# Causal mask on the tensor engine, q scaled before it is turned, and half of an output projection between heads

## The chip, the cores and the metric

The kernel runs on one core of a Trainium2 chip. The metric is the device time of one execution in microseconds (us). Five engines work side by side, each in its own fixed order of instructions: PE (matrix products and transposes), DVE (elementwise operations and reductions), ACT (activations and copies), POOL (elementwise operations) and SP (here it only issues DMAs). They wait for each other by semaphores. SBUF is the on-chip memory, PSUM the accumulator memory in banks of 2 KB a partition, into which PE writes. A change is timed by the median of several executions.

## The reference

The program is a trunk of two layers over x [512 tokens, 1024]. Each layer is a gated feed-forward block, a mixer, a cross attention to 256 memory tokens and another feed-forward block. The change touches layer 1's mixer alone:

```python
def _mla_mixer(h, positions, w_in, q_lora_g, kv_lora_g, w_uq, w_ukv, q_g, k_g, w_out):
    c_q, c_kv, k_r = jnp.split(h @ w_in, [512, 768], axis=-1)
    q = (_rmsnorm(c_q, q_lora_g) @ w_uq).reshape(b, s, 16, 96)
    kv = (_rmsnorm(c_kv, kv_lora_g) @ w_ukv).reshape(b, s, 16, 64 + 64)
    k_nope, v = kv[..., :64], kv[..., 64:]
    k = jnp.concatenate([k_nope, broadcast(k_r)], axis=-1)   # 64 + 32
    q = _rmsnorm(q, q_g); k = _rmsnorm(k, k_g)               # per head, over 96
    ... # rope on the last 32 of q and k
    sc = q @ k.T * 96 ** -0.5
    p = softmax(where(k_pos <= q_pos, sc, -inf))
    return (p @ v).reshape(b, s, 1024) @ w_out
```

There are 16 heads of 96 (q, k) and 64 (v) columns. The result is added to x, and the cross attention follows.

## The kernel before, in words

x lives feature-major on the chip, as eight tiles [128, 512]. Every large product runs as three passes of PE (lines 97 to 100, `mm3`): each operand is split into a high part, rounded to the multiplier's width (type fp32r), and a low part; the passes are high by high, low by high and high by low. Weights come in granules by DMA from SP's queue (L89); ACT makes their high part (L79), POOL or DVE the low part (L83).

**Layer 1's attention** is `mla_attn`. The 16 heads are in four groups of four. A group's projections are eight steps: four of q, one for each tile of 128 tokens (`proj_q`: a product of 384 columns into one of two banks "A", a copy, the squares on ACT at L681, their sums on DVE at L682), then four of k and v (`proj_kv`, 512 columns). After the last step come the sums' inverse roots (`rsqrt`), the scale of q by token and head (`sqr`, L663), and the normalized k (`ks`, L638 and L639; on DVE for group 0, on POOL for the others). 14 of the 32 steps run before the first head, the rest as filler between the parts of the heads, where the table FILL says how many steps stand at each of three places of a head.

**The loop over n = 0..16** does, in this order on PE: the scores of head n in three units of query blocks (512, then 384 + 128, then 256 columns; three PSUM banks "lg"); the transposes of head n-1's weights, units 0 and 1; filler; the transposes of unit 2; the turn of q and k for head n+2 (`turn`: four transposes each, L703); filler; the product with v (`values`, L808); filler. All transposes write one of two PSUM banks "pt". A bank is free again when it has been copied out: the weights' units 0 and 1 (wT0, wT1) by ACT at L795, unit 2 (wT2) by DVE at L797, q and k by both engines.

**A head's softmax**: DVE adds the mask to the diagonal blocks in PSUM (L760), reduces each row to its negative maximum (L765), multiplies that by the token's scale of q (L767); ACT takes the exponential with that scale and bias and sums the rows (L771); DVE inverts the sums (L773) and scales the rows (L777).

A scheduler sets the order of the instructions on each engine when the program is built, by its own costs. On PE the code fixes the order in addition (`queued`): what a part issues comes behind what was issued before it.

**The output projection** (`out_proj`) follows the loop: four pairs of output tiles, each pair in two halves of the contraction (o's tiles 0 to 3, then 4 to 7; one such tile holds two heads), 24 PE passes a half; then x += the result (L194), and the next norm's split and squares. The squares of the memory's tokens and its split (the next stage's preparation) are spread into the same time.

Of the kernel before, what the change touches and what calls it, by code (L numbers as in the profile page):

```python
# [8 lines left out]
F32R = mybir.dt.float32r  # L9
I32 = mybir.dt.int32  # L10
AF = mybir.ActivationFunctionType
ALU = mybir.AluOpType
# [14 lines left out]
class Trunk:  # L27
    """The residual stream xT lives feature-major on chip; every product runs as
    three fp32r passes over operands split exactly into a high and a low part."""

    def __init__(self, ctx, tc, a, stop=None):
# [10 lines left out]
        # PSUM: two banks stay through all phases, which start in their own banks and end in these two,  # L42
        # so that no phase's first product waits for the last one's evacuation
# [3 lines left out]
    def queued(self):  # L47
        """What the block issues on the tensor engine comes behind what it had before."""
        return self.tc.issue_after(self.pe.ins)
# [9 lines left out]
    # ---------------------------------------------------------------- pieces  # L59
    def constants(self):  # L60
# [3 lines left out]
        # the first weights ahead of x: their split takes longer  # L64
# [10 lines left out]
    def split(self, hi, lo, src, eng_hi="act", eng_lo="dve"):  # L75
        """hi = src rounded to the multiplier's width, lo = src - hi (exact)."""
# [8 lines left out]
    def gran(self, src, kt, cols, lo="pool"):  # L85
        """A weight granule [128, kt*cols] loaded and split."""
# [15 lines left out]
    def rsqrt(self, ssq, n, scale, eps, shape=None):  # L102
        """1/sqrt(ssq*scale + eps) on [128, n] by bit estimate and three Newton steps."""
# [13 lines left out]
    def prep(self, g, f):  # L117
        """Split gain*x_f for the next norm's consumers."""
# [12 lines left out]
    def squares(self, f):  # L131
        """Add the squares of x_f to the sums of the next norm."""
# [9 lines left out]
    def stats(self, pp, tag, bufs=None, bc=False):  # L142
        """rstd of every token: rc [128, NT] by token tile, and, if bc, rbc broadcast over partitions."""
# [28 lines left out]
    def out_half(self, ps, w, src, kh, first):  # L172
        """One half of the contraction of a pair of out_proj's output tiles, in steps."""
        wh, wl = self.gran(w, 4, 256)
        for m in range(2):
            for k in range(4):
                c = slice(m * P, (m + 1) * P)
                self.mm3(ps[m], (wh[:, k, c], wl[:, k, c]), src[4 * kh + k], first and k == 0, not first and k == 3)
                yield

    def out_proj(self, pp, tag, w, src, order, g, begun=None):
        """x += src @ w by pairs of output tiles; w in granules [pair*2 + khalf] of [128, 4, 256].
        begun: accumulators that hold the first half already."""
        nc = self.nc
        for mp in range(4):
            if begun and mp in begun:
                ps = begun[mp]
            else:
                ps = [self.psA() if mp in (0, 3) else self.t(pp, [P, S], tag) for _ in range(2)]
                self.run_all(self.out_half(ps, w[mp * 2 + order[0]], src, order[0], True))  # L190
            self.run_all(self.out_half(ps, w[mp * 2 + order[1]], src, order[1], False))
# [7 lines left out]
    # ---------------------------------------------------------------- FFN  # L199
# [43 lines left out]
    # ---------------------------------------------------------------- token-major products  # L243
    def tok_chunk(self, pp, tag, grans):
        """h @ w for 256 columns, token-major: two banks of [128, 2, 256]."""
# [11 lines left out]
    # ---------------------------------------------------------------- layer 0's mixer  # L257
# [15 lines left out]
    def sgu(self, p, pp, v, og):  # L273
# [8 lines left out]
        # only s <= t mixes: partition s, free t  # L282
# [50 lines left out]
    def stick(self, p, pp, v, ob, src):  # L333
        """Stick-breaking attention, scores as [key, query]: causal blocks only."""
        nc, a = self.nc, self.a
        # key block -> (unit, column of its queries j*128.. in the unit); units are one bank each
# [9 lines left out]
        # -1 where row key >= column key  # L346
# [3 lines left out]
        # far below every score where key >= query: no softplus there, and no weight  # L350
# [762 lines left out]
```

## Time and profile before

| | |
|---|---|
| median of 3 runs | 2326.71 us (2326.22 to 2329.08) |
| the profiled execution's span | 2328.0 us |
| PE / DVE / ACT / POOL busy | 98% / 44% / 38% / 39% of the span |
| granted TensorE clock in the stretches of layer 1's attention | 1.00 |
| layer 1's attention and its projections | about 1580 to 1750 us |
| output projection behind it, to its last pass | 1750 to 1783.6 us |

Times in rows are us from the start of the span, unless marked ns. A row of an instruction gives start, duration, engine, line, operation, output <- inputs, partitions and elements; in brackets the idle time of its engine before it and what ended it. A row of a group gives the count, the busy time in us with the mean of one in ns, and the idle time before the group's instructions. The windows give, for each stretch, its length, each engine's busy time with the count of its instructions, the granted clock, the DMA share and GB/s. A matmul's duration runs to its modelled end, so consecutive ones overlap in the rows: what one costs PE is the distance from its start to the next start.

### The profile page before, as it was taken

Reading aid. Unit: us, or ns where it says so; the run is one execution under the profiler, and the core shown is the slowest. Engines: PE = TensorE matmul, PEld = TensorE weight load, DVE = VectorE, ACT = ScalarE, POOL = GpSimd, SP = SyncE. Lnnn points to the kernel's source line nnn. Section 1 sums busy time; section 2 is a strip of 40 time slices with the busy share of each in tenths; the row PEclk is TensorE's granted clock in tenths of the full one; section 3 lists DMA queues with packets and bytes.
Section 4 is the critical chain, followed back from the end, with each engine's and each line's share of the span. In section 5 each row is a group of like instructions: output and inputs, shape, how many; then the busy total and the mean of one; then the engine's idle time right before and its main releaser. Section 6 shows DMA issues by size and latency. Waiting matters only on the chain. (4 is left out here: it accounts for less than half of the span.)

```text
span 2328.0 us, 28369 instructions
## 1 busy us (share of the span) xinstructions
PE 2274.4 (98%) x11152; PEld 1891.5 (81%) x11152; DVE 1018.2 (44%) x1830; ACT 875.1 (38%) x1448; POOL 903.4 (39%) x441
## 2 busy tenths in 40 slices
PE   7999999999999999999999999998999999999999
PEld 6888888977988788888878888897768887888887
DVE  5322433465745533133343133368886545430330
ACT  4222233355644332232332223346655443322321
POOL 4444444201242444444544444434212323445443
PEclk9999999999999999999999999999999999999999
DMA  4223323311431232332322332321103313323322
GB/s 152 92 87 113 92 82 118 92 46 47 134 110 55 83 99 81 110 100 83 108 90 83 108 100 86 99 80 57 37 19 119 127 55 91 91 79 111 100 81 92
DMA packets 67350, 208.65 MB, mean 90 GB/s; under 512 B 8592, under 2 KB 10640, under 8 KB 67216
## 3 DMA queue, kind: packets, MB, share of 16 engines
q1 hardware_dynamic: 67216, 206.83, 29.1%
q8 instruction: 88, 1.44, 0.3%
q14 instruction: 46, 0.38, 0.1%
HBM read 204.70 MB, written 2.10 MB: 89 GB/s over the span
## 5 line engine op out<-in xcount | busy, mean ns | idle before, releaser
L83 POOL TENSOR_TENSOR wl<-wr,wh 128x1024 fp32r<-128x1024 f32 (+2 forms) x382 | 850.6, 2227 | 1253.0 <-ACT wh L79 1188.8
L79 ACT CAST wh<-wr 128x1024 fp32r<-128x1024 f32 (+3 forms) x423 | 408.7, 966 | 1029.8 <-PE mm L99 540.7
L98 PE MATMUL mm<-hh,wh 128*128 128x512 f32 x1440 | 562.8, 391 | 6.6 <-ACT hh L125 6.6
L100 PE MATMUL mm<-hh,wl 128*128 128x512 f32 x1440 | 562.5, 391 | 0.9 <-POOL wl L83 0.9
L99 PE MATMUL mm<-hl,wh 128*128 128x512 f32 x1440 | 562.2, 390 | 0.5 <-DVE hl L126 0.5
L98 PEld LDWEIGHTS mm<-hh,wh 128*128 128x128 f32 x1440 | 271.5, 189 | 62.9 <-ACT hh L125 6.6
L100 PEld LDWEIGHTS mm<-hh,wl 128*128 128x128 f32 x1440 | 271.6, 189 | 57.6 <-POOL wl L83 1.3
L99 PEld LDWEIGHTS mm<-hl,wh 128*128 128x128 f32 x1440 | 271.3, 188 | 57.6 <-DVE hl L126 1.0
L98 PE MATMUL A<-ah,wh 128*128 128x512 f32 x704 | 277.4, 394 | 0.0
L100 PE MATMUL A<-ah,wl 128*128 128x512 f32 x704 | 276.0, 392 | 0.0
L99 PE MATMUL A<-al,wh 128*128 128x512 f32 x704 | 273.2, 388 | 0.0
L222 DVE TENSOR_TENSOR t<-mm,rbc 128x512 f32<-128x512 f32 x88 | 60.8, 691 | 390.5 <-PE mm L100 390.5
L234 DVE SCALAR_TENSOR_TENSOR x<-A,x 128x512 f32<-128x512 f32 x64 | 44.3, 691 | 354.3 <-PE A L100 354.3
L83 DVE TENSOR_TENSOR al<-t,ah 128x512 fp32r<-128x512 f32 x88 | 160.8, 1828 | 59.1 <-ACT ah L79 59.1
L100 PEld LDWEIGHTS A<-ah,wl 128*128 128x128 f32 x704 | 132.1, 188 | 31.0
L99 PEld LDWEIGHTS A<-al,wh 128*128 128x128 f32 x704 | 132.2, 188 | 29.6
L98 PEld LDWEIGHTS A<-ah,wh 128*128 128x128 f32 x704 | 132.3, 188 | 26.4
L220 DVE TENSOR_TENSOR t<-mm,rbc 128x512 f32<-128x512 f32 x88 | 60.9, 692 | 117.1 <-PE mm L100 110.8
L126 DVE SCALAR_TENSOR_TENSOR hl<-x,gc,hh 128x512 fp32r<-128x512 f32 x64 | 82.8, 1307 | 36.7 <-ACT hh L125 36.6
L98 PE MATMUL A<-hh,wh 128*128 128x512 f32 x224 | 91.6, 410 | 0.7 <-ACT hh L79 0.7
L99 PE MATMUL A<-hl,wh 128*128 128x512 f32 x224 | 90.0, 402 | 0.0
L100 PE MATMUL A<-hh,wl 128*128 128x512 f32 x224 | 89.8, 401 | 0.0
(322 smaller groups left out, 3260.6 us busy)
## 6 DMA issues: line engine op xcount, KB each, us to landing
wr<-in_w_gu SPq DMA_DIRECT2D x176, 512.0 KB, 3.6
wr<-in_w_dn SPq DMA_DIRECT2D x64, 384.0 KB, 3.1
wr<-in_w_dn SPq DMA_DIRECT2D x64, 320.0 KB, 2.9
wr<-in_xmem_wkv SPq DMA_DIRECT2D x32, 512.0 KB, 3.2
wr<-in_xmem_wq SPq DMA_DIRECT2D x16, 512.0 KB, 3.3
wr<-in_xmem_wo SPq DMA_DIRECT2D x16, 512.0 KB, 3.2
wr<-in_sbg_w_zv SPq DMA_DIRECT2D x12, 512.0 KB, 3.5
wr<-in_sbg_w_qk SPq DMA_DIRECT2D x8, 512.0 KB, 3.6
```

Of the source, the lines that this page charges most:

```text
L79: nc.scalar.copy(out=hi, in_=src)
L83: e.tensor_tensor(out=lo, in0=src, in1=hi.bitcast(F32), op=ALU.subtract)
L98: mm(out, lhsT=A[0], rhs=B[0], start=start, stop=False, skip_group_check=True)
L99: mm(out, lhsT=A[0], rhs=B[1], start=False, stop=False, skip_group_check=True)
L100: self.pe = mm(out, lhsT=A[1], rhs=B[0], start=False, stop=stop, skip_group_check=True)
L126: nc.vector.scalar_tensor_tensor(out=hl, in0=self.x[f], scalar=col, in1=hh.bitcast(F32), op0=ALU.mult, op1=ALU.subtract)
L220: nc.vector.tensor_tensor(out=t1, in0=pg, in1=self.rbc, op=ALU.mult)
L222: nc.vector.tensor_tensor(out=t2, in0=pu, in1=self.rbc, op=ALU.mult)
L234: nc.vector.scalar_tensor_tensor(out=self.x[m], in0=ps, scalar=0.5, in1=self.x[m], op0=ALU.mult, op1=ALU.add)
```

## The change

1. **Mask.** In each unit of scores the last pass no longer ends the accumulation; one more matmul adds the mask to the diagonal blocks: lhsT is the mask [128, 128], rhs the identity repeated over the unit's blocks (128, 256 and 128 columns), both of type fp32r, one pass (L782). The addition on DVE goes.
2. **q's scale.** After a group's ks, POOL multiplies all of the group's q, 128 x 1536, by the scale (L672). The multiplication of the maxima on DVE (L767) goes, and so does the exponential's scale operand.
3. **Half of the output projection.** After the 32 projection steps the filler goes on with 32 more: the first half (o's tiles 0 to 3) of all eight output tiles, in the two banks "A", each added to x by DVE when it is done (L747). FILL has (2, 0, 2) for n = 9 to 16. The output projection behind the loop does the second halves alone.

```diff
-        FILL = [(0, 1, 1)] + [(1, 0, 1)] * 8 + [(0, 0, 0)] * 8
+        FILL = [(0, 1, 1)] + [(1, 0, 1)] * 8 + [(2, 0, 2)] * 8
...
             knorm(st, y[:, 0], nc.vector if g == 0 else nc.gpsimd)
+            nc.gpsimd.tensor_tensor(out=st["qs"], in0=st["qs"], in1=st["s"][:, :, :, None].to_broadcast([P, NT, G, 96]),
+                                    op=ALU.mult)
...
+        def first_half():
+            for mp in range(4):
+                ps = [self.psA() for _ in range(2)]
+                for i, _ in enumerate(self.out_half(ps, a["mla_w_out"][mp * 2], o, 0, True, True)):
+                    if i % 4 == 3:
+                        f = 2 * mp + i // 4
+                        tt(out=self.x[f], in0=self.x[f], in1=ps[i // 4], op=ALU.add)
+                    yield
...
-                    self.mm3(z[:, c0:c0 + wd], (qh[:, c], ql[:, c]), (kh[:, 0:wd], kl[:, 0:wd]), x == 0, True)
+                    self.mm3(z[:, c0:c0 + wd], (qh[:, c], ql[:, c]), (kh[:, 0:wd], kl[:, 0:wd]), x == 0, False)
...
-                tt(out=d, in0=d, in1=neg[:, None, :].to_broadcast([P, n_, P]), op=ALU.add)
+                self.pe = nc.tensor.matmul(d, lhsT=neg[0], rhs=neg[1][:, None, :].to_broadcast([P, n_, P]), start=False,
+                                           stop=True, skip_group_check=True)
...
-                tt(out=nm[:, ii], in0=nm[:, ii], in1=s_[:, ii, h], op=ALU.mult)
...
-                    nc.scalar.activation(out=pt[:, c0:c0 + wd], in_=z[:, c0:c0 + wd], func=AF.Exp, scale=s_[:, i, h:h + 1],
+                    nc.scalar.activation(out=pt[:, c0:c0 + wd], in_=z[:, c0:c0 + wd], func=AF.Exp,
...
-                self.out_proj(pp, "mm", a["mla_w_out"], o, (0, 1), 5)
+                self.out_proj(pp, "mm", a["mla_w_out"], o, (0, 1), 5, {mp: None for mp in range(4)})
```

(In `mla_attn` of the changed kernel `neg` is the pair identity, mask; ks is made at L645 and L646, sqr at L670, the exponential stands at L793, the copies wT0 and wT1 at L817, wT2 at L819.)

How the order of instructions moves is seen at three places. **DVE at group 0**, before the first head: the end of the inverse roots, sqr, the two halves of ks and the next sum of q's squares. Before:

```order
L114 SCALAR_TENSOR_TENSOR rs_y_12159<-rs_u_12161,rs_y_12159 128x32
L663 TENSOR_SCALAR sqr_12171<-rs_y_12159 128x16
L638 TENSOR_TENSOR ks_12173<-kn_12107,rs_y_12159 128x16x64
L639 TENSOR_TENSOR ks_12173<-krr_11512,rs_y_12159 128x16x32
L682 TENSOR_REDUCE ssqk_12189<-prs_12221 128x4
```

This order is the same after the change, under other line numbers. **POOL at that place**, after the change:

```order
L83 TENSOR_TENSOR wl_12275<-wr_12272,wh_12274 128x1024
L83 TENSOR_TENSOR wl_12496<-wr_12493,wh_12495 128x768
L672 TENSOR_TENSOR qs_12025<-qs_12025,sqr_12175 128x1536
L83 TENSOR_TENSOR wl_12502<-wr_12499,wh_12501 128x768
L699 TENSOR_TENSOR qr_2113_12263<-qs_12193,rt0c_1979_11448 128x256
```

L672 is new there: it stands between the low parts of two weight granules of 128x768 and needs sqr. Before, the two granules follow each other. **ACT in one of the later heads**: the four exponentials of a head (L771, pb by lg), the two copies of the weights of the head before it (wT) and the turn of q and k. Before:

```order
L771 ACTIVATE pb_2471_13707,asm_13701<-lg_13702,anm_13700,sqr_13443 128x512
L795 COPY wT_2477_13746<-pt_13741 128x512
L795 COPY wT_2479_13753<-pt_13748 128x512
L771 ACTIVATE pb_2473_13721,asm_13701<-lg_13713,anm_13700,sqr_13443 128x384
L771 ACTIVATE pb_2473_13721,asm_13701<-lg_13713,anm_13700,sqr_13443 128x128
L771 ACTIVATE pb_2475_13735,asm_13701<-lg_13730,anm_13700,sqr_13443 128x256
L79 CAST qTh_13765<-pt_13760 96x512
L710 ACTIVATE kTh_13774<-pt_13769,gqk_1989_11493 96x512
```

After:

```order
L793 ACTIVATE pb_2483_13734,asm_13728<-lg_13729,anm_13727 128x512
L793 ACTIVATE pb_2485_13747,asm_13728<-lg_13739,anm_13727 128x384
L793 ACTIVATE pb_2485_13747,asm_13728<-lg_13739,anm_13727 128x128
L793 ACTIVATE pb_2487_13760,asm_13728<-lg_13755,anm_13727 128x256
L817 COPY wT_2489_13770<-pt_13765 128x512
L817 COPY wT_2491_13777<-pt_13772 128x512
L79 CAST qTh_13795<-pt_13790 96x512
L719 ACTIVATE kTh_13804<-pt_13799,gqk_1989_11493 96x512
```

The two copies have moved from behind the first exponential to behind the fourth. **PE in head n = 14**: the last transposes of the weights of units 0 and 1, unit 2, the product with v and the next head's scores. Before:

```order
L790 MATMUL pt_13917<-ident_100,pb_2495_13807 128x128
L790 MATMUL pt_13917<-ident_100,pb_2493_13793 128x128 x2
L790 MATMUL pt_13924<-ident_100,pb_2495_13807 128x128
L790 MATMUL pt_13924<-ident_100,pb_2493_13793 128x128
L808 MATMUL av_13864<-wT_2520_13915,vs_13264 64x512
```

After:

```order
L812 MATMUL pt_13969<-ident_100,pb_2507_13843 128x128
L812 MATMUL pt_13969<-ident_100,pb_2505_13830 128x128 x2
L98 MATMUL A_13876<-hh_2215_12665,wh_13879 128x512
L99 MATMUL A_13876<-hl_2216_12666,wh_13879 128x512
L100 MATMUL A_13876<-hh_2215_12665,wl_13880 128x512
L98 MATMUL A_13876<-hh_2274_12898,wh_13879 128x512
L99 MATMUL A_13876<-hl_2275_12899,wh_13879 128x512
L100 MATMUL A_13876<-hh_2274_12898,wl_13880 128x512
L812 MATMUL pt_13982<-ident_100,pb_2507_13843 128x128
L812 MATMUL pt_13982<-ident_100,pb_2505_13830 128x128
L830 MATMUL av_13912<-wT_2537_13967,vs_13247 64x512
```

Six passes of the output projection (A by the attention's output, hh and hl) now stand ahead of unit 2's two transposes, and six more stand behind the product with v. In the order before, two of the later heads had no such filler; in the others the scheduler had put passes of the first pair of output tiles, 45 of its 48 in all, between the heads' parts.

More of the change, by code (lines that the diff above doesn't have):

```diff
@@ L170, in run_all, with out_half @@
             pass
-    def out_half(self, ps, w, src, kh, first):
+    def out_half(self, ps, w, src, kh, first, last=False):
         wh, wl = self.gran(w, 4, 256)
@@ L177, in out_half @@
                 c = slice(m * P, (m + 1) * P)
-                self.mm3(ps[m], (wh[:, k, c], wl[:, k, c]), src[4 * kh + k], first and k == 0, not first and k == 3)
+                self.mm3(ps[m], (wh[:, k, c], wl[:, k, c]), src[4 * kh + k], first and k == 0, last and k == 3)
                 yield
@@ L185, in out_proj @@
         for mp in range(4):
-            if begun and mp in begun:
-                ps = begun[mp]
-            else:
+            ps = begun.get(mp) if begun else None
+            if ps is None:
                 ps = [self.psA() if mp in (0, 3) else self.t(pp, [P, S], tag) for _ in range(2)]
+            added = bool(begun) and mp in begun and begun[mp] is None
+            if not (begun and mp in begun):
                 self.run_all(self.out_half(ps, w[mp * 2 + order[0]], src, order[0], True))
-            self.run_all(self.out_half(ps, w[mp * 2 + order[1]], src, order[1], False))
+            self.run_all(self.out_half(ps, w[mp * 2 + order[1]], src, order[1], added, True))
             for m in range(2):
@@ L546, in mla @@
                                     channel_multiplier=1)
+            negr = self.t(op, [P, P], "cnegr", F32R)
+            idr = self.t(op, [P, P], "identr", F32R)
+            nc.scalar.copy(out=negr, in_=neg)
+            nc.scalar.copy(out=idr, in_=self.ident)
             cT = [(self.t(op, [P, S], f"ch{f}", F32R), self.t(op, [P, S], f"cl{f}", F32R)) for f in range(6)]
@@ L556, in mla @@
                     tc.tile_pool(name="mlaps", bufs=1, space=bass.MemoryType.PSUM) as pp:
-                self.mla_attn(p, pl, pp, cT, krr, skr, gqk, neg, tq, o)
+                self.mla_attn(p, pl, pp, cT, krr, skr, gqk, (idr, negr), tq, o)
             with tc.tile_pool(name="mlops", bufs=4, space=bass.MemoryType.PSUM) as pp:
-                self.out_proj(pp, "mm", a["mla_w_out"], o, (0, 1), 5)
+                self.out_proj(pp, "mm", a["mla_w_out"], o, (0, 1), 5, {mp: None for mp in range(4)})
     def lora(self, p, pp, c, n, ss, cT, lg, j0):
@@ L729, in filler, with both @@
                     yield
-        fill = filler()
+        def first_half():
[6 more added lines that the diff above has]
+                    yield
+        def both():
+            yield from filler()
+            yield from first_half()
+        fill = both()
         def take(n, queue=True):
@@ L736, in take @@
                     with self.queued():
-                        next(fill)
+                        next(fill, None)
                 else:
-                    next(fill)
+                    next(fill, None)
         def scores(n, qk):
@@ L747, in scores @@
             sm = self.t(p, [P, NT], "asm", bufs=2)
-            s_ = gs[g]["s"]
             for u, blks in enumerate(((3,), (2, 0), (1,))):
```

## The prediction

> **What bounds the kernel now.** I read the page's engine table first, then the windows over layer 1's attention, then PE's waits there.
>
> The page's head and first table (time, share, instructions):
>
> ```profile
> span 2328.0 us, 28369 instructions
> PE 2274.4 (98%) x11152; PEld 1891.5 (81%) x11152; DVE 1018.2 (44%) x1830; ACT 875.1 (38%) x1448; POOL 903.4 (39%) x441
> ```
>
> PE is busy for 98% of the span: each matmul added costs its own time, unless it falls into one of PE's few gaps. Busy time by stretches of 20 us:
>
> ```profile
> 1560.00:1580.00 20.00, 15.27 (x76) 12.58 (x76) 16.27 (x38) 12.03 (x35) 6.23 (x3) 1.00 0.22 66
> 1580.00:1600.00 20.00, 18.13 (x103) 15.88 (x102) 15.08 (x38) 12.91 (x26) 10.27 (x9) 1.00 0.21 66
> ...
> 1740.00:1760.00 20.00, 18.97 (x80) 12.72 (x80) 9.01 (x23) 10.18 (x23) 5.87 (x4) 1.00 0.20 60
> 1760.00:1780.00 20.00, 20.00 (x89) 16.54 (x89) 13.68 (x19) 12.99 (x22) 6.97 (x7) 1.00 0.37 125
> sum 220.00, PE 205.09 PEld 157.29 DVE 172.16 ACT 140.80 POOL 64.81; mean PE 18.64 PEld 14.30 DVE 15.65 ACT 12.80 POOL 5.89
> ```
>
> The sum is over eleven stretches: PE idles 220 - 205.1 = 14.9 us, of which 4.7 lie before 1580, where nothing changes. The change can win back at most 10.2 us. DVE is the fullest of the others, with a mean of 15.65 a stretch against ACT's 12.80. What ended PE's idle time from 1580 to 1750 (total, times, longest):
>
> ```profile
> PE pt L703 <- DVE wT L797: 3.8, 6, 1.7
> PE pt L790 <- ACT wT L795: 3.0, 4, 1.2
> PE A L98 <- ACT hh L79: 0.7, 1, 0.7
> ```
>
> So 6.8 us are waits for copies of transposed weights, which stand late on DVE and ACT: a transpose needs one of two "pt" banks, and the copy frees it.
>
> **Masks on PE.** DVE loses two groups (times in us, mean in ns):
>
> ```profile
> L760 DVE TENSOR_TENSOR lg<-lg,cneg 128x128 f32<-128x128 f32 (+1 forms) x48 | 15.3, 334 | 6.6 <-PE lg L100 6.6
> L767 DVE TENSOR_TENSOR anm<-anm,sqr 128x1 f32<-128x1 f32 (+1 forms) x48 | 11.3, 244 | 0.1
> ```
>
> That is 26.6 us of DVE. PE gains three masks a head, of 128, 256 and 128 columns. The nearest rows are the scores themselves, of the same widths and type:
>
> ```profile
> 1698.08 0.22 PE L98 MATMUL lg<-kTh,qTh 96*128 96x128 f32 x1
> 1698.14 0.27 PE L99 MATMUL lg<-kTl,qTh 96*128 96x128 f32 x1
> 1698.26 0.27 PE L100 MATMUL lg<-kTh,qTl 96*128 96x128 f32 x1
> 1698.37 0.34 PE L98 MATMUL lg<-kTh,qTh 96*128 96x256 f32 x1
> 1698.54 0.28 PE L99 MATMUL lg<-kTl,qTh 96*128 96x256 f32 x1
> 1698.66 0.29 PE L100 MATMUL lg<-kTh,qTl 96*128 96x256 f32 x1
> 1698.78 1.04 PE L790 MATMUL pt<-ident,pb 128*128 128x128 f32 x8
> ```
>
> From start to start 128 columns take 0.06 to 0.12, mean (1698.37 - 1698.08)/3 = 0.10; 256 columns 0.12 to 0.17. A head's masks cost 0.10 + 0.12 + 0.10 = 0.32, sixteen heads **5.1 us**. Bounds: 16 x (0.06 + 0.12 + 0.06) = 3.8; a 128-column pass as dear as the dearest 256 (0.17 each) 8.2. The middle is nearest, since a mask stands in the same chain of matmuls.
>
> [...]
>
> **q scaled ahead.** Four POOL multiplications of 128x1536 replace 48 tiny DVE ones. Prices on POOL, and the least, median and largest time of DVE's sqr, which stands next to POOL's work for three groups and alone for group 0:
>
> ```profile
> L638 POOL TENSOR_TENSOR ks<-kn,rs_y 128x1024 f32<-128x1024 f32 x3 | 5.7, 1908 | 11.8 <-DVE rs_y L114 11.8
> L639 POOL TENSOR_TENSOR ks<-krr,rs_y 128x512 f32<-128x512 f32 x3 | 3.1, 1050 | 0.0
> L663 DVE TENSOR_SCALAR sqr<-rs_y x4: 176/1760/1912, 1585.0 to 1695.2; 128x16 f32<-128x16 f32 x4
> ```
>
> 512 columns more cost 1908 - 1050 = 0.86 us, so 1536 cost about 1.91 + 0.86 = 2.77 us. POOL itself has room (5.89 of 20 busy, the sum row). But a DVE operation on SBUF beside a POOL operation takes ten times its own time: 1.76 to 1.91 against 0.18. For groups 1 to 3 the new operation stands behind two POOL operations already there, and q is needed more than 2 us later; I put these at 0. Group 0 is different. There DVE makes ks itself, POOL stands idle, and the new operation is released by sqr, one instruction ahead of ks. These rows follow sqr:
>
> ```profile
> 1585.10 1.22 DVE L638 TENSOR_TENSOR ks<-kn,rs_y 128x1024 f32<-128x1024 f32 x1
> 1586.23 0.69 DVE L639 TENSOR_TENSOR ks<-krr,rs_y 128x512 f32<-128x512 f32 x1
> 1586.83 0.55 DVE L682 TENSOR_REDUCE ssqk<-prs 128x4 f32<-128x384 f32 x1
> 1587.41 0.49 ACT L681 ACTIVATE prs<-A 128x384 f32<-128x384 f32 x1 [1.58 <-DVE ssqk L682]
> 1587.96 0.49 PE L98 MATMUL A<-wh,ch 128*128 128x512 f32 x1 [0.52 <-ACT prs L681]
> 1588.76 0.40 PE L98 MATMUL A<-wh,ch 128*128 128x512 f32 x1
> 1588.99 0.39 PE L99 MATMUL A<-wl,ch 128*128 128x512 f32 x1
> ```
>
> Does POOL get in between two DVE operations that stand back to back? Here it did:
>
> ```profile
> 1627.66 0.47 DVE L777 TENSOR_SCALAR pb<-pb,asm 128x512 f32<-128x512 f32 x1
> 1627.91 0.81 POOL L693 TENSOR_TENSOR qs<-qr,qr 128x256 f32<-128x256 f32 x1
> 1628.05 0.68 DVE L767 TENSOR_TENSOR anm<-anm,sqr 128x2 f32<-128x2 f32 x1
> ```
>
> L767's 0.15 became 0.68, and it ended when POOL did. So at group 0 POOL's scaling would start as the first half of ks ends (1586.3) and hold the second half back until 1589.1, 2.8 us late. Behind it on DVE waits the reduction L682, for that ACT's L681, for that PE's next projection, which already waits 0.52 there: no cover. Price **2.8 us**; bounds 0 (DVE's second half goes first and POOL waits) and 2.8.
>
> [...]
>
> **Copies behind the exponentials.** On ACT the copies wT0 and wT1 came behind the first exponential of a head, and now come behind all four (the order in the change's section). Means by shape (busy us, mean ns):
>
> ```profile
> L765 DVE TENSOR_REDUCE anm<-lg 128x1 f32<-128x512 f32 x16 | 10.9, 684 | 0.2
> L771 ACT ACTIVATE pb<-lg,anm,sqr 128x512 f32<-128x512 f32 x16 | 12.5, 781 | 18.7 <-DVE anm L767 18.7
> L771 ACT ACTIVATE pb<-lg,anm,sqr 128x384 f32<-128x384 f32 x16 | 10.7, 668 | 2.3 <-DVE anm L767 2.1
> L771 ACT ACTIVATE pb<-lg,anm,sqr 128x256 f32<-128x256 f32 x16 | 9.0, 561 | 1.7 <-DVE anm L767 1.7
> L771 ACT ACTIVATE pb<-lg,anm,sqr 128x128 f32<-128x128 f32 x16 | 7.2, 449 | 0.0
> L795 ACT COPY wT<-pt 128x512 f32<-128x512 f32 x32 | 17.1, 590 | 8.8 <-PE pt L790 8.8
> ```
>
> One late head, from its first score: unit 0 takes three 512-column passes (0.23 each, 1588.76 to 1588.99) and its mask, 0.8. About 0.25 later DVE reduces for 0.68: first exponential at 1.8. The four take 0.78 + 0.67 + 0.45 + 0.56 = 2.46, so wT0 starts at about 4.3 and frees its bank at 4.85. PE: three units with masks 2.2, eight transposes 0.8 (1698.78, 0.10 each), two filler steps of three passes 1.4: ready at 4.4 to 4.65. It stalls 0.2 to 0.45 before the last two transposes, and 0.27 more before q's turn, which needs wT1. That is 0.5 to 0.7 in each head, 8 to 11.5 us in sixteen, in place of 6.8 + 0.7 (the wait for hh falls under the filler at the end). Change: +0.5 to +4; taken **+2**. The scheduler took DVE's relief and gave it to the exponentials, not to the copies that PE waits for.
>
> **Half of the output projection.** 96 matmuls move forward, none is added. In the order of before 45 of the first pair's 48 stood in these heads already (two heads had none), so most gaps had work near and were waits for banks, not for want of products. Eight more additions of x on DVE, read from PSUM, at 0.69 each (5.5 us) fall in a stretch that lost 26.6. Value 0. Behind attention the stretch that covers the next norm and the memory's preparation gets shorter by 54 matmuls, 54 x 0.23 = 12.4 us. There now:
>
> ```profile
> 1750.00:1784.00 34.00, 34.00 (x151) 28.20 (x152) 21.57 (x31) 20.56 (x36) 12.84 (x10) 1.00 0.38 124
> ```
>
> DVE's 21.6 and ACT's 20.6 fitted in 34 us and must now go into 21.6. The memory's products, which need no norm, stand behind as more cover; I take 0, with 3 us as the other end.
>
> **Sum.** 5.1 + 2.8 + 2 + 0 = +9.9 us. The profiled execution's span is 2328.0, 1.3 above the median of the runs, 2326.71: by span 2337.9, as a median **2336.6**.
>
> **Rivals.**
> (A) The stalls go. DVE's 26.6 us make every softmax early enough, the copies come before PE is due, and at group 0 DVE goes first: 5.1 - 6.8 - 0.7 = -2.4, 2324.3. The place is the pt banks; it decides if the fourth exponential ends before 3.8 in a head (4.4 less 0.59 for a copy). For it: 6.6 us of idle ahead of L760's masks, a DVE that is ahead of PE. Against: ACT's order. Not slower; chance 0.22. With masks at the low bound and 9.7 of the 10.2 idle us gone: 3.8 - 9.7 = -5.9, 2320.8; chance 0.06.
> (B) No collision at group 0: 5.1 + 2 = 7.1, 2333.8. For it: only one example of POOL getting in is quoted, with a short operation. Chance 0.17.
> (C) The cover behind attention is too short: 9.9 + 3, 2339.6. For it: 20.6 of ACT's work into 21.6; against: PE is at 20.00 of 20 from 1760 on with products to spare. Chance 0.13.
> That the change doesn't move what it says is answered by the order.
>
> **Numbers.** The forecast has 0.42. No change that can be told is within 0.2%, 4.65 us: 2322.1 to 2331.4. Rival A's first form lies in it, and the low tail of the forecast and B (masks 3.8, stalls +0.5, no collision: 2331.0) adds 0.02: same 0.24. Faster is A's second form, 0.06; slower the rest, 0.70. The likeliest case's own range is 2331 to 2341. To hold 8 in 10 the range goes down to 2323.5 (half of A) and up to 2341.5 (C, or masks at 8.2).
>
> **What would show it.** Masks: 48 matmuls from lg starts with spacing 0.10 to 0.12 each. Group 0: an L646 on DVE of over 3 us, and PE's wait for prs longer than 3 us. Stalls: PE waits "pt <- ACT wT" in most heads, each under 0.5, and "pt <- DVE wT" smaller than 3.8. Tail: PE without a gap behind 1760. I'm wrong if waits for wT sum to under 3 us, if L646 takes 0.69, or if a wait opens that isn't named here (an A bank held by the new additions, DVE standing behind POOL in groups 1 to 3).

## The result

The change makes the kernel slower. The median is 2353.15 us (2349.68 to 2360.0, four runs) against 2327.89 us, a ratio of 1.0108 with a 95% interval of 1.0091 to 1.0126. The direction was forecast. The size was not: +25 us in place of +10, outside the range. The profiled execution has a span of 2358.3 us; it is the slowest of the four, so its parts add up to 30 us, not 25.

The page's first table after:

```profile
span 2358.3 us, 28399 instructions
PE 2294.5 (97%) x11200; PEld 1905.2 (81%) x11200; DVE 1010.8 (43%) x1742; ACT 870.8 (37%) x1450; POOL 915.3 (39%) x445
```

PE is busy 20.1 us longer with 48 matmuls more. 48 matmuls of 0.1 us explain 5. The windows over layer 1's attention show where the rest is (columns as before; the third figure from the right is the granted clock):

```profile
1580.00:1600.00 20.00, 15.56 (x85) 13.64 (x84) 13.79 (x27) 11.16 (x26) 11.73 (x9) 1.00 0.13 40
...
1620.00:1640.00 20.00, 17.25 (x90) 12.51 (x89) 14.21 (x31) 13.26 (x34) 8.49 (x8) 0.90 0.17 54
1640.00:1660.00 20.00, 19.51 (x101) 14.43 (x99) 10.99 (x27) 9.30 (x26) 2.39 (x1) 0.93 0.00 0
1660.00:1680.00 20.00, 17.68 (x88) 12.71 (x89) 11.56 (x37) 11.05 (x29) 5.62 (x3) 0.91 0.08 27
1680.00:1700.00 20.00, 17.17 (x90) 12.64 (x89) 11.95 (x25) 10.82 (x29) 9.17 (x8) 0.91 0.16 53
1700.00:1720.00 20.00, 16.80 (x78) 10.80 (x77) 14.38 (x38) 10.11 (x26) 7.56 (x4) 0.91 0.08 27
1720.00:1740.00 20.00, 19.32 (x106) 13.94 (x105) 12.71 (x31) 10.40 (x26) 2.80 (x2) 1.00 0.09 27
```

From 1620 to 1720 two things are new. In four of the five stretches PE idles 2.3 to 3.2 us, where before it idled at most 2.1 in any of them. And the granted clock is 0.90 to 0.93 in all five, where it was 1.00 before in every stretch: a busy PE that runs slower. From 1720 on, in the late heads, neither is there. What ended PE's idle time, from 1560 to 1800:

```profile
PE pt L812 <- ACT wT L817: 7.2, 12, 2.4
PE pt L712 <- DVE wT L819: 6.1, 4, 2.4
PE A L98 <- ACT prs L690: 3.1, 1, 3.1
...
PE pt L712 <- ACT wT L817: 1.0, 2, 0.5
```

The waits for copies of weights are 14.3 us in place of 6.8. Four of them are of 1.6 to 2.4 us, one each in heads 3, 5, 7 and 9 (head n is here the stretch from its first score to the next head's; the first head is 0). Head 3, row by row (start, duration, engine, line):

```profile
1634.24 2.34 POOL L83 TENSOR_TENSOR wl<-wr,wh 128x1024 fp32r<-128x1024 f32 x1
...
1634.46 2.26 DVE L799 TENSOR_SCALAR pb<-pb,asm 128x256 f32<-128x256 f32 x1
...
1636.65 0.41 DVE L819 COPY wT<-pt 128x256 f32<-128x256 f32 x1
...
1637.12 1.09 PE L712 MATMUL pt<-ident,ks 128*96 128x128 f32 x4 [2.37 <-DVE wT L819]
...
1638.13 4.53 PE L830 MATMUL av<-wT,vs 128*64 128x512 f32 x8
```

POOL splits a weight granule. DVE's last scaling of pb takes 2.26 us beside it (0.35 at 1675.02, with POOL idle) and ends 0.14 us after it, and the copy of wT2 stands behind the scaling. In the order of before, the copy came behind the first of the four scalings, ahead of the other three. PE waits 2.37 us for the bank. Then the product with v takes 4.53 us for its eight matmuls; undisturbed it takes 2.37 (a row of the forced order below). The reason is in the windows of 2 us over the same place:

```profile
1632.00:1634.00 2.00, 1.66 (x8) 0.91 (x6) 1.96 (x5) 2.00 (x9) 1.84 (x3) 1.00 0.59 219
1634.00:1636.00 2.00, 0.70 (x5) 0.39 (x4) 1.97 (x3) 1.37 (x5) 2.00 (x2) 0.98 0.00 0
1636.00:1638.00 2.00, 0.88 (x4) 0.64 (x4) 1.98 (x4) 0.00 (x0) 1.31 (x2) 0.50 0.22 45
1638.00:1640.00 2.00, 2.00 (x4) 0.62 (x4) 0.75 (x1) 0.68 (x1) 0.00 (x0) 0.50 0.62 225
1640.00:1642.00 2.00, 2.00 (x5) 0.82 (x4) 0.00 (x0) 0.00 (x0) 0.00 (x0) 0.50 0.00 0
1642.00:1644.00 2.00, 2.00 (x9) 1.42 (x8) 0.00 (x0) 0.00 (x0) 0.00 (x0) 0.81 0.00 0
```

The clock is at half from 1635.94 on, while PE still waits, and stays there for 6.83 us. So this stall is paid twice: once as idle time, once as slow work afterwards.

Head 7 repeats this: the scaling takes 2.26 us from 1687.19, beside a split of 2.34 from 1686.96, PE waits 2.44, and half clock follows for 3.41. Heads 5 and 9 come to their stall by another way. Head 5:

```profile
1656.60 2.39 POOL L83 TENSOR_TENSOR wl<-wr,wh 128x1024 fp32r<-128x1024 f32 x1 [19.29 <-ACT wh L79]
...
1656.76 2.27 DVE L106 TENSOR_SCALAR rs_v<-ssqk 128x32 f32<-128x32 f32 x1
...
1659.92 0.58 ACT L793 ACTIVATE pb<-lg,anm 128x384 f32<-128x384 f32 x1 [2.47 <-DVE rs_u L112]
...
1661.47 0.44 PE L812 MATMUL pt<-ident,pb 128*128 128x128 f32 x2 [1.64 <-ACT wT L817]
```

Here it is rs_v, a link in the group's inverse roots, that takes 2.27 us beside POOL's split and ends 0.04 us after it (0.17 at 1609.25, with POOL idle). DVE's maxima stand behind it, so ACT's second exponential waits 2.47 us (the row names the operation of the roots that ended last ahead of it), and the copy of wT0, which now stands behind three exponentials, comes late with it. In head 9 rs_v takes 2.26 and ACT waits 2.46.

**Where 30 us went** in the profiled execution, by the distance between the same events in both traces:

| stretch | before | after | difference |
|---|---|---|---|
| up to PE's sum of squares ahead of layer 1's mixer (L147; "the event" below) | 1530.25 | 1532.60 | +2.4 (there already at 1202 us, far ahead of the change) |
| from there to the first score | 64.13 | 66.70 | +2.6 |
| first score to the memory's first product | 189.25 | 209.36 | +20.1 |
| from there to the sum of the memory's squares | 5.77 | 5.77 | 0 |
| from there to the end | 538.56 | 543.86 | +5.3 |

The 20.1 are, first, the masks: the distance from a head's first score to the next transpose of weights is 1.91 before and 2.22 after (two rows of before, then two of after).

```profile
1676.83 0.40 PE L98 MATMUL lg<-kTh,qTh 96*128 96x512 f32 x1
...
1678.74 0.93 PE L790 MATMUL pt<-ident,pb 128*128 128x128 f32 x7
```

```profile
1628.61 0.40 PE L98 MATMUL lg<-kTh,qTh 96*128 96x512 f32 x1
...
1630.83 1.05 PE L812 MATMUL pt<-ident,pb 128*128 128x128 f32 x8
```

0.31 by sixteen heads is 5.0 us. Then 14.3 - 6.8 = 7.5 us of waits for wT, less the 0.7 for hh, which is gone; and the clock, 7.3 us (one minus the granted clock, times PE's busy time, summed over windows of 5 us). 5.0 + 6.8 + 7.3 = 19.1 of 20.1. The last 5.3 are nearly all behind attention: a new wait of 1.38 us for x's squares at 1816.31, and half clock for 6.83 us from 1816.85, which costs 3.4.

The start of attention shows the collision that was forecast:

```profile
1587.45 1.22 DVE L645 TENSOR_TENSOR ks<-kn,rs_y 128x1024 f32<-128x1024 f32 x1
...
1587.62 3.66 POOL L672 TENSOR_TENSOR qs<-qs,sqr 128x1536 f32<-128x1536 f32 x1 [2.70 <-DVE sqr L670]
...
1588.59 3.24 DVE L646 TENSOR_TENSOR ks<-krr,rs_y 128x512 f32<-128x512 f32 x1
...
1592.87 0.49 PE L98 MATMUL A<-wh,ch 128*128 128x512 f32 x1 [3.09 <-ACT prs L690]
```

The second half of ks took 3.24 us in place of 0.69, and PE waited 3.09 in place of 0.52: 2.6 us each. Of POOL's 3.66 (2.75 for each of the other three groups) the first 1.05 lie beside the first half of ks. No half clock lies in this stretch, before or after, so the 2.6 us are the collision's.

### The profile page after: what moved, and what is told of

It reads as the page before. It is cut to its first block, busy times and chain, and to the rows that moved or that the text cites. A ratio compares the mean times of both kernels' runs of the same rounds, so it can differ in the third digit from the quotient of the medians.

```text
span 2358.3 us, 28399 instructions
## 1 busy us (share of the span) xinstructions
PE 2294.5 (97%) x11200; PEld 1905.2 (81%) x11200; DVE 1010.8 (43%) x1742; ACT 870.8 (37%) x1450; POOL 915.3 (39%) x445
## 5 line engine op out<-in xcount | busy, mean ns | idle before, releaser
L98 PE MATMUL A<-hh,wh 128*128 128x512 f32 x240 | 98.7, 411 | 0.0
L99 PE MATMUL A<-hl,wh 128*128 128x512 f32 x240 | 95.2, 397 | 0.0
L100 PE MATMUL A<-hh,wl 128*128 128x512 f32 x240 | 95.1, 396 | 0.0
```

The lines of the kernel that those rows point to most:

```text
L98: mm(out, lhsT=A[0], rhs=B[0], start=start, stop=False, skip_group_check=True)
L99: mm(out, lhsT=A[0], rhs=B[1], start=False, stop=False, skip_group_check=True)
L100: self.pe = mm(out, lhsT=A[1], rhs=B[0], start=False, stop=stop, skip_group_check=True)
```

## The experiments

Theory 1: the loss beyond the masks' own time comes from the order that the scheduler makes of the change. The softmax no longer waits for DVE's mask, so it comes first, and the copies that free the transposes' banks come last; there they stand behind DVE operations that take 2.3 us beside POOL's, as in heads 3 and 7 above; and half clock follows the four stalls of 1.6 to 2.4 us, 7.3 us of loss. The rivals are named in the expectations. Each kernel's median stands beside the kernel before on the same chip, whose median was 2328.79, 2330.22 and 2329.96 in the three groups of four.

### One part at a time

**Mask on PE alone.** From the change, FILL's last eight rows are (0, 0, 0) again, the output projection is whole, and q's scale is applied in the softmax.

```diff
-        FILL = [(0, 1, 1)] + [(1, 0, 1)] * 8 + [(2, 0, 2)] * 8
+        FILL = [(0, 1, 1)] + [(1, 0, 1)] * 8 + [(0, 0, 0)] * 8
...
-            nc.gpsimd.tensor_tensor(out=st["qs"], in0=st["qs"], ...)
...
+                tt(out=nm[:, ii], in0=nm[:, ii], in1=s_[:, ii, h], op=ALU.mult)
```

> The kernel before with one part: the mask added by PE (q's scale and the output projection as before). Theory 1 (the masks' own time, and the copies of the weights pushed behind the softmax on DVE and ACT, where a POOL operation can hold them): in this kernel's order wT2 stands behind three or four scalings of pb on DVE, wT1 behind the exponentials on ACT. So +5 for the masks, and one to four stalls of about 2.4 us with PE at half clock behind them: +10 to +16 us, 2337 to 2343. Rival 2 (the filler of the output projection is the cause): +5, 2332. Rival 3 (PE is throttled because it is denser, whatever the order): +5 and a clock as low as in the whole change, without stalls above 2 us.

Measured: 2357.88 us, ratio 1.0128 (1.0113 to 1.0143): +29 us, more than the whole change. PE's waits from 1580 on:

```profile
PE pt L710 <- ACT wT L817: 10.5, 10, 1.7
PE pt L710 <- DVE wT L819: 6.6, 5, 1.9
PE pt L812 <- ACT wT L817: 3.7, 4, 2.5
```

20.8 us of waits for these banks, and 7.2 us of half clock. Rival 2 (the filler) and rival 3 (a clock that falls without stalls) are out: no filler is here, and each half clock of the loop (five, of 3.4 us) follows a stall. The loss was larger than theory 1 said. wT1 stands behind all exponentials, and each of these waits for the small multiplication by q's scale (L789), which POOL holds too in heads 5 and 9: it takes 2.32 and 2.29 us there, 0.15 when free. How much of the loss this makes was not tried by itself.

**q scaled ahead alone.**

```diff
+            nc.gpsimd.tensor_tensor(out=st["qs"], in0=st["qs"], in1=st["s"][:, :, :, None].to_broadcast([P, NT, G, 96]), op=ALU.mult)
...
-                tt(out=nm[:, ii], in0=nm[:, ii], in1=s_[:, ii, h], op=ALU.mult)
```

> The kernel before with one part: q scaled ahead on POOL. Theory 1: the order of the copies stays as before; only group 0's second half of ks waits for POOL, +2.6 us at the start of attention; the removed DVE multiplications give back 0 to 2: +1 to +4, 2328 to 2331. Rival 4 (POOL's new operations hold DVE in every group): +8 or more, with a DVE operation of over 2.5 us beside each of four.

Measured: 2328.50 us, ratio 1.0000 (0.9991 to 1.0010). The first score stands 66.81 us behind the event, +2.7. But this trace has half clock for 3.41 us from 1577.72, worth 1.7, where the kernel before has none, and PE's wait for prs is 1.66 in place of 0.52; so the +2.7 are not the collision alone (the table under "Group 0's scaling of q on DVE" compares like with like). The heads are 1.3 us shorter (152.59 against 153.89 from the first score to the last product with v). The collision itself is there in this kernel too:

```profile
1584.37 3.67 POOL L668 TENSOR_TENSOR qs<-qs,sqr 128x1536 f32<-128x1536 f32 x1 [2.70 <-DVE sqr L666]
...
1585.34 3.25 DVE L642 TENSOR_TENSOR ks<-krr,rs_y 128x512 f32<-128x512 f32 x1
```

Rival 4 (a hold in every group) is out: no stall of over 1.7 us in the heads, and no DVE operation of over 2.4 there; the two of 2.4 stand beside weight splits, not beside q's scaling.

**Half of the output projection alone.** From the change, the mask is added by DVE and q's scale is applied in the softmax, as before.

```diff
-                self.pe = nc.tensor.matmul(d, lhsT=neg[0], rhs=neg[1][:, None, :].to_broadcast([P, n_, P]), ...)
+                tt(out=d, in0=d, in1=neg[:, None, :].to_broadcast([P, n_, P]), op=ALU.add)
...
-            nc.gpsimd.tensor_tensor(out=st["qs"], in0=st["qs"], ...)
...
+                tt(out=nm[:, ii], in0=nm[:, ii], in1=s_[:, ii, h], op=ALU.mult)
```

> The kernel before with one part: half of the output projection as filler. Theory 1: the order of the copies stays; the filler covers some waits for pt banks (up to -3), the shorter cover behind attention costs about what the change's trace shows from the sums of squares on (+5.3, of which about 3 are half clock): -2 to +5, 2325 to 2332. Rival 2 (the filler is the main cause: its additions on DVE and its A banks hold PE): +12 to +20.

Measured: 2333.10 us, ratio 1.0017 (1.0008 to 1.0026), +4, 1 us above the range expected. The heads don't gain: the waits for wT are 8.2 us, one of 2.45 that is followed by half clock. And behind attention PE now waits for the last squares of x, which the longer output projection covered before:

```profile
1793.59 1.05 PE L147 MATMUL at<-ones,sqs 128*128 128x1 f32 x8 [1.38 <-DVE sqs L140]
```

Half clock follows here as well (3.41 us at half speed cost 1.7): 3.1 us. All six kernels with this part have the wait (1.3 to 1.4 us) and half clock behind it, five of them for 3.41 us, the change for 6.83.

**Mask and q's scale, without the filler.**

```diff
-        FILL = [(0, 1, 1)] + [(1, 0, 1)] * 8 + [(2, 0, 2)] * 8
+        FILL = [(0, 1, 1)] + [(1, 0, 1)] * 8 + [(0, 0, 0)] * 8
...
-                self.out_proj(pp, "mm", a["mla_w_out"], o, (0, 1), 5, {mp: None for mp in range(4)})
+                self.out_proj(pp, "mm", a["mla_w_out"], o, (0, 1), 5)
```

> The change without its third part: mask on PE and q scaled ahead. Theory 1: masks +5, group 0 +2.6, the loop's stalls with the clock behind them +10 to +14: +17 to +22, 2344 to 2349. Rival 2: +8, 2335.

Measured: 2350.05 us, ratio 1.0096 (1.0081 to 1.0111): +21, 1 us above the range expected. The third part adds 3 to it, not the bulk. The parts don't add up (29 + 0 + 4 against 25): q's scale ahead takes back some of what the mask loses.

### The order of the copies

**Mask alone, softmax written behind the copies.** The scores of a head are issued as before. The code of its softmax stands behind the transposes and copies of the head before it, so that the scheduler ranks those first.

```diff
                 with self.queued():
-                    pb = scores(n, qk.pop(0))
+                    zs = scores(n, qk.pop(0))
...
                     weights(old, wT, (2,))
+            if n < 16:
+                pb = softmax(n, zs)
```

> Mask on PE alone, as in p_mask, but the code writes a head's softmax behind the copies of the weights of the head before it, so that the scheduler ranks the copies first: on ACT wT0 and wT1 follow the first exponential, on DVE wT2 stands one to three scalings earlier. Nothing else differs, PE's order is the same. Theory 1 (the order of the copies is the loss): waits for wT fall from 21.8 us to below 10, no stall above 2 us and no half clock: +5 to +9, 2334 to 2338 in place of p_mask's 2358. Theory 5 (the 48 masks on PE are dear in themselves): stays at 2350 or above.

Measured: 2337.29 us, ratio 1.0040 (1.0025 to 1.0055): +7 where the same instructions in the other order cost +29.

```profile
PE pt L818 <- ACT wT L823: 4.1, 3, 1.7
PE pt L710 <- DVE wT L825: 3.5, 3, 2.4
```

7.6 us of waits in place of 20.8 (1.5 for sums come in), and 1.6 us of half clock in place of 7.2. POOL still holds a DVE operation for 1.9 to 2.5 us in each of heads 3, 5, 7 and 9; with the copies ahead, these heads' waits for wT are 0, 1.6, 0.2 and 1.7 us, in place of 3.4, 4.2, 3.2 and 2.5. One of the details failed: a stall of 2.39 was left, in head 1, with half clock behind it. Rival 5 (masks dear in themselves) is out.

**The whole change, softmax written behind the copies.**

> The whole change with the softmax written behind the copies. On ACT the copies now follow the second exponential in place of the fourth, on DVE wT2 moves ahead of one or two scalings. Theory 1: the loop's waits fall from 14.3 us towards 7 and most half clocks go: 2353 becomes 2338 to 2345 (masks 5, group 0's start 2 to 3, the tail behind the output projection 2 to 5). Theory 5: 2350 or above.

Measured: 2349.48 us, ratio 1.0093 (1.0076 to 1.0110). Only 3 to 4 us better than the change, and the two intervals overlap: the expectation failed. In the order, wT0 and wT1 still stand behind two exponentials, and wT2 behind two scalings in most heads:

```profile
PE pt L712 <- DVE wT L825: 11.8, 13, 3.6
```

ACT's copies account for 3.3 more. So the edit had moved the late copy from ACT to DVE. It left open whether the order could do it at all; hence the next one.

**The whole change, order forced.** On ACT the exponentials of units 1 and 2 come behind wT0 and wT1, on DVE the scalings of pb behind wT2, by an explicit edge in every head.

```diff
+                late = n > 0 and u > 0
...
+                    with (self.tc.issue_after(self.cA.ins) if late else nullcontext()):
                       nc.scalar.activation(out=pt[:, c0:c0 + wd], in_=z[:, c0:c0 + wd], func=AF.Exp,
...
+                    with (self.tc.issue_after(self.cV.ins) if n > 0 else nullcontext()):
                       ts(out=pt[:, c0:c0 + wd], in0=pt[:, c0:c0 + wd], scalar1=sm[:, i:i + 1], ...)
```

> The whole change with the order of the copies forced: on ACT the exponentials of units 1 and 2 stand behind wT0 and wT1, on DVE the four scalings of pb behind wT2, in every head. Theory 1 (what the change loses beyond the masks' time is copies late behind the softmax, and PE's half clock that follows long quiet stretches): waits for wT fall from 14.3 us to below 6, half clock within the loop from 7 us lost to below 2: 2336 to 2342. Rival 7 (group work on DVE and POOL makes the stalls whatever the copies' place, as the 15 us of waits left in the version with the softmax written later suggest): 2346 or above, stalls of over 2 us at heads 5 and 9.

Measured: 2338.52 us, ratio 1.0040 (1.0025 to 1.0055). This kernel does all that the change does, with no instruction more or less, and is 15 us faster. Its waits, and a product with v at full clock:

```profile
PE pt L712 <- DVE wT L828: 8.2, 9, 2.0
PE A L98 <- ACT prs L690: 1.7, 1, 1.7
...
PE pt L821 <- ACT wT L826: 0.5, 1, 0.5
```

```profile
1687.56 2.37 PE L839 MATMUL av<-wT,vs 128*64 128x512 f32 x8
```

The waits for wT came to 8.7, not below 6, two of them of 1.70 and 2.02, at the heads that rival 7 names. But no half clock is left in the loop, and some 15 of the change's 25 us went with the order. Of the other 10, the masks are 5.0, group 0's start 2.7 (the first score stands 66.88 behind the event, 64.13 before) and the tail 2 to 3 (540.60 from the sum of the memory's squares to the end, 538.56 before): 9.7 to 10.7, for a measured 8.6. Of the 2.7, 1.7 are half clock from 1577.97, ahead of group 0's scaling, as in q scaled ahead alone; a run without it would show another split. And the forced order lets q's scaling on POOL hold a scaling of pb for 2.78 us in each of groups 1 to 3, which happened in none of them in the change.

### POOL's share

**All group work of layer 1 on DVE.**

```diff
-            knorm(st, y[:, 0], nc.vector if g == 0 else nc.gpsimd)
-            nc.gpsimd.tensor_tensor(out=st["qs"], in0=st["qs"], ...)
+            knorm(st, y[:, 0], nc.vector)
+            nc.vector.tensor_tensor(out=st["qs"], in0=st["qs"], ...)
...
-                st["wkv"] = self.gran(a["mla_w_ukv"][g], 2, 512)
+                st["wkv"] = self.gran(a["mla_w_ukv"][g], 2, 512, lo="dve")
```

(likewise the granules of q's projection and the rope of q)

> The whole change with all of layer 1's group work on DVE in place of POOL: ks, q's scale, the rope of q, and the low parts of the projections' weights. Nothing on POOL but the low parts of the output projection's granules can hold a DVE operation then; DVE gets some 30 us more work. Theory 1 (the stalls of 2.4 us are DVE operations that wait for POOL): no DVE operation of over 2 us between heads 1 and 8, the stalls at heads 3 and 7 go, group 0's wait for prs shrinks to about 1 to 2; 2338 to 2347. Rival 6 (the order of the copies alone, without POOL, makes the stalls): 2350 or above, stalls stay at 2.4.

Measured: 2349.55 us, ratio 1.0092 (1.0077 to 1.0107). The stall of head 3 is gone, as theory 1 says; but heads 5, 7 and 9 became longer (20.0, 16.0 and 15.8 us from first score to first score, where the change has 15.6, 14.7 and 14.4), with DVE's own group work in front of the softmax and the copies:

```profile
PE pt L812 <- ACT wT L817: 10.1, 11, 3.6
PE pt L712 <- DVE wT L819: 6.1, 4, 4.2
```

The edit didn't keep POOL out of these three heads. The splits of the output projection's granules, which stayed on POOL, hold DVE in each of them ahead of the softmax: rs_v in head 5 and again in head 9 (2.33), and in head 7 two products of the rope (2.29 and 2.60, 0.41 when free):

```profile
1642.54 2.38 POOL L83 TENSOR_TENSOR wl<-wr,wh 128x1024 fp32r<-128x1024 f32 x1 [99.69 <-DVE anm L788]
...
1642.64 2.31 DVE L106 TENSOR_SCALAR rs_v<-ssqk 128x32 f32<-128x32 f32 x1
```

So it isn't shown whether DVE's 30 us of added work or what is left of POOL makes these stalls. The expectation failed, and neither theory 1 nor rival 6 is settled by this kernel alone. One thing came out that was not expected: the first score stands 59.73 us behind the event, 4.4 less than in the kernel before. Between the event and the first score four DVE operations are held by POOL's splits in the kernel before (1.7 to 2.1 us each), and one here.

**Group 0's scaling of q on DVE.**

```diff
-            nc.gpsimd.tensor_tensor(out=st["qs"], in0=st["qs"], ...)
+            (nc.vector if g == 0 else nc.gpsimd).tensor_tensor(out=st["qs"], in0=st["qs"], ...)
```

> The whole change with group 0's scaling of q on DVE behind ks, in place of POOL (groups 1 to 3 as before). Theory 1: L646 is back at 0.7 us, but DVE does the 128x1536 itself, about 1.7 us; PE's wait for prs falls from 3.1 to 1.5 to 2; 1 to 2 us faster than the change, 2350 to 2353. Rival (the wait has another cause): no change in the wait.

Measured: 2350.47 us, ratio 1.0088 (1.0073 to 1.0103). This is in the range expected, but the interval overlaps the change's. The wait for prs fell to 0.5 and L646 is short again, but the first score stands 66.81 us behind the event, no earlier than in the change. The reason lies mostly ahead of group 0's scaling: this trace has half clock for 6.83 us from 1573.31, behind PE's wait of 3.0 us for prk, and the change's has none. That wait is the same in eleven of the kernels; seven traces have half clock behind it. Sorted by it, the distance from the event to the first score is:

| half clock ahead of group 0 | q not scaled ahead | q scaled on POOL | q scaled on DVE |
|---|---|---|---|
| none | 64.13 (before, and half of the projection alone), 64.15 (before with the softmax behind the copies) | 66.70 (the change) | |
| 3.41 us | | 66.81 (scale alone), 66.79 (softmax behind the copies), 66.88 (order forced) | |
| 6.83 us | 65.98 (mask alone), 65.90 (the same, softmax behind the copies) | 67.93 (mask and scale) | 66.81 (this kernel) |

Within a row, the scaling ahead costs 2.0 to 2.6 us on POOL (one trace in each row) and 0.9 on DVE (one trace). On DVE the waits move to the turn of the first heads (kTl, 1.2), but most of the price goes.

### Versions meant to beat both

**best2**: the mask on DVE and the whole output projection, as in the kernel before; q scaled ahead, group 0 on DVE; the softmax written behind the copies; the low parts of the weights of the projections ahead of the heads on DVE.

```diff
-                st["wkv"] = self.gran(a["mla_w_ukv"][g], 2, 512)
+                st["wkv"] = self.gran(a["mla_w_ukv"][g], 2, 512, lo="dve" if g == 0 else "pool")
...
-                st["wq"] = [self.gran(a["mla_w_uq"][2 * g + i], 2, 384) for i in range(2)]
+                st["wq"] = [self.gran(a["mla_w_uq"][2 * g + i], 2, 384, lo="dve" if g < 2 else "pool") for i in range(2)]
```

> A version to beat both: the mask on DVE and the output projection as before; q scaled ahead (group 0 on DVE); the softmax written behind the copies; and the low parts of the weights for group 0's and 1's projections that run ahead of the heads on DVE, so that POOL holds no DVE operation there. Theory 1: the start of attention gains 3 to 4.4 us (as in the version without POOL), the loop 1 to 2: 2320 to 2325. If POOL's share was not the cause of the start's wait: 2327.

**best3**: the same with the order of the copies forced, by the edges shown above.

> As best2, with the order of the copies forced in every head as in the forced version of the change. Theory 1: as best2 or 1 to 3 us better, 2318 to 2324. If forcing makes the exponentials late enough to stall the next head's weights: slower than best2, with waits for pb.

Measured: best2 2326.36 us, ratio 0.9984 (0.9974 to 0.9993); best3 2323.11 us, ratio 0.9972 (0.9961 to 0.9983). best3's first score stands 60.80 us behind the event (64.13 before), its heads take 151.42 us (153.89 before). best2 has 61.82 and 154.18, with 1.7 us of half clock in its heads; it missed its range by 1.4 us. Its 0.16% is within what the prediction counted as no change, best3's 0.28% just outside.

**The kernel before with the softmax written behind the copies**, nothing else:

> The kernel before with the softmax written behind the copies, nothing else. Theory 1: the 6.8 us of waits for wT shrink by 0 to 4: 2323 to 2328. If it is slower, the copies' rank delays the exponentials enough to make a wait of its own.

Measured: 2327.47 us against 2330.22, ratio 0.9991 (0.9981 to 1.0000). The waits for wT fall from 6.8 to 3.1, and 1.9 us of a wait for pb come in: the gain is at the edge of what can be told.

## Why the prediction was right or wrong

**The masks: right.** 5.1 forecast, 5.0 measured (0.31 a head for 0.32).

**Group 0: right in size and in the rows**, L646 at 3.24 us and the first score 2.6 late in the change, without half clock there. The other kernels with the scaling on POOL agree once half clock ahead of it is set apart (2.0 in the one with a partner), and with the product on DVE 0.9 are left: the price is mostly POOL's hold, as the step says.

**An ordinary late head: right.** The walk had wT0 free at 4.85 from the first score and 0.5 to 0.7 us of stall. In head 10 wT0 runs from 4.30 to 4.89, unit 2's transposes stand at 4.94 and the turn at 5.52; heads 10 to 13 are 10.2 to 10.3 us long.

**The step that failed is "Copies behind the exponentials", +2 us.** It walked through one ordinary late head and multiplied by sixteen. In heads 3, 5, 7 and 9 POOL splits a weight granule, the hold by POOL that the step before used for group 0 meets DVE again, and the stall is 1.6 to 2.4 us, not 0.5 to 0.7: heads of 14.4 to 15.6 us beside neighbours of 10.3 to 11.2. In heads 3 and 7 the held operation is the last scaling of pb, and behind it stands wT2, which had moved on DVE and which the step didn't price at all. In heads 5 and 9 it is rs_v, ahead of the maxima: the exponentials come late, and with them ACT's copies, which the step had start at 4.3 in every head (wT0 starts at 6.4 in these two). The kernel before has such holds in the same four heads (1.7 to 1.8 us, at 1629.3, 1646.1, 1673.2 and 1689.3), and only head 5 has a wait of over 0.5 us for wT there, of 1.70; new is what stands behind them. The prediction named "DVE standing behind POOL in groups 1 to 3" among the things that would make it wrong; its price of 0 was for POOL's new operations, which in the change hold nothing in these groups, and it had no price for the old splits. The waits for wT came to 14.3 us; the step's upper end was 6.8 + 0.7 + 4 = 11.5.

**A term was missing: the clock.** The trace of before had no half clock in this stage, and a stall was priced at its own length; elsewhere that trace does have it, 6.83 us from 1834.89, behind a quiet stretch of 4.65. In the change's trace half clock stands four times in the loop, behind quiet stretches of 4.48 to 4.93 us, and costs 7.3 us; the forced order has none of it.

**The value 0 behind attention failed, and rival C happened beside the forecast's own terms**: 1.4 us of wait for the squares, and half clock behind it for 3.4 us in the change's trace, 1.7 in the five others with this part. The rival's 3 has no half clock in it; that 1.4 + 1.7 comes near it is luck.

With the order forced the change comes to a ratio of 1.0040, some 9 us: the forecast's +9.9 was close to what the change costs without the late copies of the group heads, and 15 us short of what it costs with them. The closeness is partly luck: its +2 for the copies is not among the 5.0, 2.7 and 2 to 3 that were measured there, and a tail and half clock are, which it put at 0. Rival A fell: the copies were later, not earlier. Rival B fell: the collision is there. The filler of the output projection was worth nothing or less, as argued.

## What to carry to other kernels

When a change relieves an engine, look at what its scheduler does with the time: here the relieved softmax overtook the copies that free the tensor engine's banks, and the order alone cost 15 us. Price a moved copy on every engine where it moves, in the heads that carry extra work, not in an ordinary one. And price a stall of PE with the half clock that may stand behind it: here four stalls of 1.6 to 2.4 us had 3.41 to 6.83 us of half clock behind each, 7.3 us of loss in all.

## What the runs showed of the hardware

**Half clock behind quiet stretches.** In the clock records of before and of the change the clock is 1.0 or 0.5, and each time at 0.5 that ends inside the span lasts 3.41 or 6.83 us (five in before, twelve in the change). I measured, in all fourteen traces from 1540 us on, the stretches of PE between two matmuls that are not transposes, and counted which were followed by half clock:

```
quiet stretch, us    no half clock   half clock
1.6 to 2.2                75              0
2.2 to 2.6                35              1
2.6 to 3.0                14             10
3.0 to 3.5                15              0
3.5 to 4.0                 1              1
4.0 to 4.5                 2              9
4.5 and more               0             24
```

(Some places stand in it once for each trace, so the counts are not independent; two stretches that lie within half clock are left out.) One place is outside the table: the wait of 1.3 to 1.4 us behind attention, followed by half clock in all six kernels that have it. It stands among twelve sums of one column each; without these as matmuls the stretch is 2.6 us (half of the projection alone). Long stretches and long stalls don't always coincide: in the change's head 5 a stall of 1.64 us among transposes (quiet for 4.59) was followed by half clock, while the place of 2.41 us with no transpose beside it (at 2002.61 in the change, where it was) was not in thirteen of fourteen traces. That is a count over traces; no run varied the stretch alone. The same stretch came with half clock behind it and without: the wait for prk ahead of group 0 makes a stretch of 3.0 us in eleven traces, and seven have half clock behind it. This may be why the change's four runs spread over 10 us where those of before spread over 3: the mean granted clock is 0.988 in the slowest and 0.992 in the fastest, and (1 - 0.988) x 2358.3 less (1 - 0.992) x 2347.9 is 9.5 us. Only the slowest has a trace.

**DVE and POOL.** DVE's elementwise operations shown above took longer beside a running POOL operation: the second half of ks 3.24 us in place of 0.69, standing back to back behind the first half; the last scaling of pb in head 3 2.26 in place of 0.35; rs_v in head 5 2.27 in place of 0.17; two products of the rope, with the group work on DVE, 2.29 and 2.60 in place of 0.41. Those that have a row above beside POOL's ended 0.03 to 0.55 us after it. Not every DVE operation on SBUF did so: in the change, a sum of prs at 1594.34 and an inversion of sums at 1687.01 lie within splits on POOL (1593.62 to 1595.47 and 1686.96 to 1689.30) and take 0.55 and 0.15 us, as elsewhere. A 128x1536 product took 2.75 us on POOL in the change (2.77 estimated) and 1.75 on DVE in best3.
